# Early factors, one place for w2's sums, and loads in another order, in a decoder block's kernel

## The chip, the core and the metric

The kernel runs on one core of one Trainium2 chip. Its time is the device time of one execution in microseconds (us), given as the median of the runs; lower is better. The core's engines are TensorE (PE, matrix products; PEld is its loading of the stationary operand), VectorE (DVE), ScalarE (ACT) and GpSimd (POOL). SyncE (SP) issues most of the transfers; POOL issues others. An engine, and each DMA queue, takes its instructions in order.

## The reference

One layer over 2048 positions of width 1024: a mixer of dilated attention heads beside a gated recurrence, and a squared-ReLU MLP of width 4096, each between two norms.

```python
h = rms_norm(x, mix_norm_pre)
z = h @ w_in                                  # q, k, v, xr, gr
attn = dilated_attention(q, k, v)             # 8 heads of 64, three dilations, softmax-weighted
rec = rg_lru(causal_depthwise_conv(xr)) * gelu(gr)
x = x + rms_norm(concat([attn, rec]) @ w_out, mix_norm_post)
h = rms_norm(x, mlp_norm_pre)
a = relu(h @ w_ff_in)
x = x + rms_norm((a * a) @ w_ff_out, mlp_norm_post)
```

All is float32. `w_ff_in` is called w1 in the kernel, `w_ff_out` w2.

## The kernel before

**Precision.** A float32 operand is split into two parts, a high one (a cast to a shorter format on ACT, line 54) and a low one (the source minus the high part, mostly on DVE, line 55). A product takes three matmuls: high by high, high by low, low by high. The names end in H and L.

**Stages.** The 2048 positions are taken in two halves of 1024. TensorE does, in this order: the projections of half 0 with its attention and the recurrence; the last projections, the products q11, q12, q13 (LATER, line 1565), 24 matmuls per tile of q, k or v; the out-projection of half 0 (OutProj, tiles m, 634 to 728 us); the MLP's first product for half 0 (mlp_in, to 1056 us); its second (mlp_out) for half 0, mixed with the attention of half 1 (`interleave`, line 1304); the remaining sets of mlp_out while w_out is loaded again; then out-projection, mlp_in and mlp_out of half 1. From the out-projection of half 0 on PE's order is written by hand; in the attention of half 1 that of ACT, DVE and SP is too. Elsewhere a scheduler with a simulated time line orders the engines; `issue_after` gives it an instruction that must come first. On PE the change moves a few transposes in LATER and nothing else.

**mlp_in** computes `h @ w1` by Strassen's scheme, seven products (m = 1 to 7) for each of 16 column groups j. Each product's left factor f_m comes from the four quarters of w1's group: 1, 2, 3, 4 are made from single quarters (3 from a difference), 5, 6, 7 are sums (line 1009). The groups go in pairs of j (mlp_in_rest, line 1081), 14 products to a pair; a product here is 12 matmuls on 128x512. The right factors are the transposed activations: hHB and hLB (high and low), hHT and hLT (sums of them). Those of the last columns are made while the first products run, and the low parts hLT then take DVE.

After a group's products the output z is squared, and A = seven sums of z (tile as, lines 1061 to 1064) is stored in DRAM; beside it w2's own sums, tile w2s (function w2_sums, lines 1070 to 1075: a load of 1 MB, four sums, a store sb of 1 MB), are computed once, 16 times in half 0. The factors of j = 0, 1 and some of j = 2 are also stored in DRAM (scr["f"], sf) in half 0 and read back in half 1, instead of being made again (line 985 and below).

**Buffers.** Rings: sh.r, four buffers of 1 MB (z as sq, the sums as, w2s, and in half 1's attention k's two parts kh and kl); sh.w, five of 512 KB (w1's raw groups w1r, x, qs and qa); sh.pair and sh.s for split parts. A load for a ring waits on its queue until the buffer's last user is done.

**mlp_out** multiplies A's sums by w2's sums: seven factors m in the order 1, 6, 5, 3, 2, 7, 4 times 16 j, each a set of 12 matmuls. A set loads a (256 KB) and b (256 KB), casts on ACT (line 1227) and subtracts on DVE (line 1229). Four sets share the buffers, in turn, and the first four lie in another pool. In interleave `fill(n)` runs n quarters of sets between pieces of the attention of half 1. There each head has qs and kh, kl, vb loaded by SP (lines 429 to 445), qa copied from qs on DVE (line 433), va loaded by POOL (eight loads of 128 KB). The join of a head pair (lines 684 to 691: two products with the weights co and an addition, per half of the columns) is on DVE for the first three pairs, on POOL for the last; its result is stored to smix, which the out-projection loads as m_0, m_4 (mix_columns, line 787).

**load_w_out** (line 746) loads w_out row block by row block (512 KB each, woL), casts it and makes the low part; in half 1 each block comes between two calls of `between`, and each call runs one set.

## Time and profile before

| | us |
|---|---|
| median of 3 runs | 2286.15 (2276.22 to 2289.51) |
| the profiled execution, its span | 2279.51, 2277.7 |
| PE busy | 2180.9 (96%) |
| DVE, ACT, POOL busy | 1511.8 (66%), 1232.6 (54%), 461.2 (20%) |
| DMA | 466.15 MB, mean 205 GB/s |

In a timeline each line is one instruction: its start, its duration, engine, line of the kernel, operation, output <- inputs, and in brackets how long its engine had been idle before it and what ended the wait. SPq is SP's queue of transfers. A row of busy time by stretches gives, for a stretch from the span's start, each engine's busy time and its instructions, then the clock that TensorE was granted (1.00 is full), the mean busy share of the 16 DMA engines, and what they moved. A row of waits gives the total, the number and the longest. Tiles are named without their numbers.

### The profile page before, as it was taken

What the parts mean: (1) busy time and instruction counts of PE and PEld (TensorE: products, weight loads), DVE (VectorE), ACT (ScalarE), POOL (GpSimd) and SP (SyncE); (2) the same over time, 40 slices, a digit from 0 to 9 for tenths busy, and PEclk for the clock granted to TensorE, in tenths of its full rate; (3) what the DMA queues carried; (4) which work ended last, traced back from release to release, by engine and by line L of the source; (5) the groups of instructions that cost most, each with busy time, mean ns of one, the idle gap of its engine ahead of it and who ended that gap; (6) DMA issues with size and microseconds to landing.
All of it is one profiled execution on the core that took longest, in us unless ns stands there. A gap on an engine that the chain in (4) does not pass through costs nothing.

```text
span 2277.7 us, 30713 instructions
## 1 busy us (share of the span) xinstructions
PE 2180.9 (96%) x10264; PEld 1782.2 (78%) x10264; DVE 1511.8 (66%) x2900; ACT 1232.6 (54%) x2489; POOL 461.2 (20%) x549
## 2 busy tenths in 40 slices
PE   8999999989999899999899999898999999999998
PEld 6678878767788677787788887777878888888887
DVE  6757465877558777774667676777775656646556
ACT  7646464644334555454666666754454545654442
POOL 5543415454013201011001010122300000000003
PEclk9999999989999999999999999999999999999999
DMA  8365675635844577769777777868454444676665
GB/s 287 94 189 176 181 232 152 197 128 183 248 159 163 208 273 284 293 228 315 220 206 219 214 234 200 217 214 238 154 206 153 167 139 156 247 252 193 193 192 181
DMA packets 217550, 466.15 MB, mean 205 GB/s; under 512 B 22464, under 2 KB 77152, under 8 KB 211120
## 3 DMA queue, kind: packets, MB, share of 16 engines
q1 hardware_dynamic: 188624, 329.52, 46.6%
q0 software_dynamic: 28768, 134.66, 16.8%
q8 instruction: 81, 1.33, 0.2%
q14 instruction: 77, 0.63, 0.1%
HBM read 329.75 MB, written 151.13 MB: 211 GB/s over the span
## 4 chain that ended last, share of the span: by engine, by line
PE 64%; DMA 10%; DVE 9%; issue 6%; ACT 5%; POOL 1%; SPq 1%; DVEq 0%; POOLq 0%; ACTq 0%
PE o L1145 8%; PE o L1144 8%; PE o L1146 8%; PE z L198 3%; PE z L199 3%; PE z L200 3%; PE za L999 3%; PE za L998 3%; PE za L1000 3%; DMA w2s<-in_dram 3%; PE m L823 2%; PE m L821 2%; PE m L822 2%; PE zc L998 2%; PE zc L999 2%
## 5 line engine op out<-in xcount | busy, mean ns | idle before, releaser
L198 PE MATMUL z<-hH,wH 128*128 128x512 f32 x640 | 263.0, 411 | 18.6 <-ACT wH L54 8.2
L199 PE MATMUL z<-hL,wH 128*128 128x512 f32 x640 | 260.8, 408 | 0.3 <-DVE hL L173 0.3
L200 PE MATMUL z<-hH,wL 128*128 128x512 f32 x640 | 259.6, 407 | 0.0
L198 PEld LDWEIGHTS z<-hH,wH 128*128 128x128 f32 x640 | 122.5, 191 | 54.6 <-DVE xr L304 9.9
L199 PEld LDWEIGHTS z<-hL,wH 128*128 128x128 f32 x640 | 122.7, 192 | 30.7 <-issue 4.3
L200 PEld LDWEIGHTS z<-hH,wL 128*128 128x128 f32 x640 | 122.9, 192 | 30.3 <-issue 4.9
L409 ACT ACTIVATE smB<-smB,stB 128x128 f32<-128x128 f32 (+3 forms) x128 | 71.6, 561 | 80.4 <-DVE stB L403 80.2
L1003 ACT ACTIVATE sq<-sq 128x512 f32<-128x512 f32 x93 | 58.8, 632 | 88.4 <-DVE sq L1007 88.3
L55 POOL TENSOR_TENSOR wL<-wraw,wH 128x512 fp32r<-128x512 f32 x58 | 82.0, 1431 | 80.7 <-ACT wH L54 77.6
L1063 POOL DMA_DIRECT2D sa<-sq x31 | 16.5, 533 | 398.0 <-ACT sq L1004 397.8
L55 DVE TENSOR_TENSOR tlB<-pT_B,thB 128x384 fp32r<-128x384 f32 x96 | 57.1, 598 | 50.1 <-ACT thB L54 46.9
L54 ACT CAST wH<-wraw 128x512 fp32r<-128x512 f32 (+1 forms) x81 | 47.1, 612 | 66.6 <-DMA wraw<-in_dram 32.5
L409 ACT ACTIVATE sm<-sm,stA 128x256 f32<-128x256 f32 (+1 forms) x128 | 63.1, 495 | 30.7 <-DVE stA L403 30.4
L1004 ACT ACTIVATE sq<-sq 128x512 f32<-128x512 f32 x124 | 76.4, 629 | 2.2
L1074 DVE TENSOR_TENSOR w2s<-w2s 128x512 f32<-128x512 f32 x64 | 44.1, 689 | 33.0 <-DMA w2s<-in_dram 32.0
L1178 POOL TENSOR_TENSOR y<-y,g4b 128x512 f32<-128x512 f32 x8 | 12.4, 1578 | 259.5 <-ACT junk_y L84 259.5
L403 DVE CUSTOM_DVE_ANT_0 smB<-SB,mask_b 128x128 f32<-128x128 f32 (+3 forms) x128 | 59.4, 483 | 6.1 <-PE pT_B L377 5.4
L55 DVE TENSOR_TENSOR tlA<-pT,thA 128x512 fp32r<-128x512 f32 (+1 forms) x64 | 42.3, 669 | 26.6 <-ACT thA L54 26.2
L54 ACT CAST thB<-pT_B 128x384 fp32r<-128x384 f32 x96 | 48.5, 510 | 19.7 <-PE pT_B L377 10.6
L607 PE MATMUL oB<-thB,vb 128*128 128x256 f32 x192 | 49.1, 285 | 9.5 <-ACT thB L54 8.9
L821 PE MATMUL m<-woH,m_0H 128*128 128x512 f32 x128 | 51.7, 404 | 5.8 <-ACT m_0H L54 5.8
L998 PE MATMUL za<-hHT,f_6H 128*128 128x512 f32 x128 | 51.3, 401 | 5.5 <-ACT sq L1037 5.4
(577 smaller groups left out, 7083.5 us busy)
## 6 DMA issues: line engine op xcount, KB each, us to landing
sa<-as POOLq DMA_DIRECT2D x32, 1024.0 KB, 6.5
w1r<-in_dram SPq DMA_DIRECT2D x58, 512.0 KB, 4.2
sa<-sq POOLq DMA_DIRECT2D x31, 768.0 KB, 4.0
wraw<-in_dram SPq DMA_DIRECT2D x79, 256.0 KB, 3.6
w2s<-in_dram SPq DMA_DIRECT2D x16, 1024.0 KB, 7.7
sb<-w2s POOLq DMA_DIRECT2D x16, 1024.0 KB, 6.8
kh<-sk SPq DMA_DIRECT2D x24, 512.0 KB, 5.1
kl<-sk SPq DMA_DIRECT2D x24, 512.0 KB, 6.9
```

What stands on the lines that cost most here:

```text
L54: return (nc.scalar.copy(out=hi, in_=src), (lo_eng or nc.vector).tensor_tensor(out=lo, in0=src, in1=f32(hi), op=ALU.subtract))
L55: (lo_eng or nc.vector).tensor_tensor(out=lo, in0=src, in1=f32(hi), op=ALU.subtract))
L198: pe.matmul(z, hi[:, k, :], hh, start=(k == 0), stop=False)
L199: pe.matmul(z, hi[:, k, :], hl, start=False, stop=False)
L200: pe.matmul(z, lo[:, k, :], hh, start=False, stop=(k == KT - 1))
L409: s.activation(out=sm[:, c0:c0 + w], in_=sm[:, c0:c0 + w], func=AF.Exp, scale=-1.0, bias=st[:, 0, u, cols[j]:cols[j] + 1], accum_out=st[:, ...
L821: pe.matmul(o, mh, wh[:, ds], start=(k == order[0]), stop=False)
L998: pe.matmul(o, hi[:, k], bh[:, k], start=start and k == 0, stop=False, skip_group_check=True)
L999: pe.matmul(o, hi[:, k], bl[:, k], start=False, stop=False, skip_group_check=True)
L1144: pe.matmul(o, ah[:, ts], bh, start=fresh and j == 0, stop=False, skip_group_check=True)
L1145: pe.matmul(o, ah[:, ts], bl, start=False, stop=False, skip_group_check=True)
L1146: pe.matmul(o, al[:, ts], bh, start=False, stop=j == NJ - 1, skip_group_check=True)
```

## The change

Seven edits, in the order of the program.

1. Half 0's factors of j = 0, 1 are made during LATER, by a generator `early_factors` that is stepped five times after each product group, and stored. Half 0's mlp_in then reads them back, as half 1's does.
2. w2's sums for j = 2 to 15 use one buffer, place[0] (once for each group), and two further ones (w2x5, w2x9) the ring sh.r. They are placed behind the last made factor of the first pair (`sh.made`). The last A of half 0 uses that place too.
3. `first_loads`: q and the high part of k of half 1's first head are loaded before the last products of mlp_in; its low part follows the masks; qa is copied before the low part is loaded; va's loads come after the last store of A (`stored`).
4. The last four sets of mlp_out are loaded 16 to 20 sets early into buffers of sh.r, where k lay.
5. The last pair's join is on DVE, and its end runs after the fourth `between`.
6. load_w_out of half 1 loads all left column halves (256 KB each), then all right ones, two halves to a `between`.
7. For half 1 x, the gains and the norm's tiles are loaded after the first columns m, whose low parts are made on DVE for t = 0.

```diff
+def first_loads(nc, sh, scr):
+    qs = sh.px.tile([P, HT], F32R, tag="w", bufs=WB, name="qs1_0")
+    nc.sync.dma_start(out=f32(qs), in_=f32(scr["q"][1][0][0].rearrange("a c t -> c a t")))
+    kh = sh.px.tile([P, 2 * HT], F32R, tag="r", bufs=RB, name="kh1_0")
+    for x in range(2):
+        nc.sync.dma_start(out=f32(kh[:, x * HT:(x + 1) * HT]), in_=f32(twice(scr["k"][x][0][0, 0])))
+    return qs, kh
...
         for a, t in ((0, kh), (1, kl)):
+            if given and a == 0:
+                continue
+            if hf and a:
+                by_runs()
...
-        if hf:
-            by_runs()
...
+                with tc.issue_after(cst["stored"].ins) if hf else contextlib.nullcontext():
+                    (g if hf else nc.sync).dma_start(out=f32(va[cs, hf + 4 * i:hf + 4 * i + 4, :]),
...
-        e = v if amid else g
+        e = v if hf else g
...
-    for k in order:
+    parts = [slice(0, TB), slice(TB, D)]
+    for x, (ds, k) in enumerate([(ds, k) for ds in parts for k in order] if hf else [(slice(0, D), k) for k in order]):
         hi, lo = wo[k]
-        between()
+        if x % 2 == 0:
+            between()
...
-        split_there(nc, hi, lo, nc.gpsimd)
+        split_there(nc, hi, lo, nc.vector if hf and t == 0 else nc.gpsimd)
...
+def early_factors(nc, sh, scr, w1, j):
+    v, g = nc.vector, nc.gpsimd
+    raw = [sh.s(f"er{j}_{i}", (P, KH, P)) for i in range(4)]
+    a11, a12, a21, a22 = raw
+    for i, t in enumerate(raw):
+        nc.sync.dma_start(out=t, in_=w1[2 * j + i // 2][:, (i % 2) * KH:(i % 2 + 1) * KH])
+    yield
+    f = {}
+    def made(m, src=None):
+        if src is None:
+            split_there(nc, *f[m])
+        else:
+            f[m] = sh.pair(f"e{j}_{m}", (P, KH, P))
+            split(nc, *f[m], src)
+        for d, t in zip(scr["f"][j, m], f[m]):
+            g.dma_start(out=d, in_=f32(t).rearrange("p k t -> p (k t)"))
+    def sub(m, x, y, op=ALU.subtract):
+        f[m] = sh.pair(f"e{j}_{m}", (P, KH, P))
+        v.tensor_tensor(out=f32(f[m][1]), in0=x, in1=y, op=op)
+    sub(5, a21, a22, ALU.add)
+    sub(7, a11, a21)
+    sub(6, f32(f[5][1]), a11)
+    v.tensor_tensor(out=a21, in0=a12, in1=f32(f[6][1]), op=ALU.subtract)
+    made(7)
...
-            if hf and kept:
+            if kept and (hf or j < 2):
                 for d, t in kept:
                     nc.sync.dma_start(out=t, in_=d)
                 return
...
-            w2_sums(v)
+            w2_sums(v, place[0])
...
-        A = sh.r(f"as{n}")
+        A = place[0] if hf == 0 and j == NJ - 1 else sh.r(f"as{n}")
...
-    def w2_sums(e):
+    def w2_sums(e, W):
         j = todo.pop(0)
-        W = sh.r(f"w2s{j}")
         nc.sync.dma_start(out=W.rearrange("p (f a) d -> p f (a d)", f=2), in_=w2[2 * j:2 * j + 2].rearrange("f p d -> p f d"))
-        sums_right(lambda o, x, y, op: e.tensor_tensor(out=o, in0=x, in1=y, op=op), *[W[:, i] for i in range(4)])
+        with tc.issue_after(sh.made.ins):
+            sums_right(lambda o, x, y, op: e.tensor_tensor(out=o, in0=x, in1=y, op=op), *[W[:, i] for i in range(4)])
         g.dma_start(out=scr["b"][j], in_=W)
...
+            if not hf and i >= len(order) * NJ - 4:
+                if x == "a":
+                    t = sh.px.tile([P, 4, TB], F32R, tag="r", bufs=RB, name=f"r{n}")
+                hi, lo = [t[:, 2 * (x == "b") + k] for k in range(2)]
...
+            for k in {len(sets) - 20: (-2, -1), len(sets) - 14: (-4, -3)}.get(i, ()):
+                made[len(sets) + k] = load(*sets[k])
+            if 5 <= i < len(sets) - 7:
                 made[i + 3] = load(*sets[i + 3])
...
+            early = [early_factors(nc, sh, scr, w1, j) for j in range(2)]
+            for step in LATER.split():
+                run(step)
+                for _ in range(5):
+                    if early and next(early[0], True):
+                        early.pop(0)
...
+                first = first_loads(nc, sh, scr)
                 run_all(end)
+                cst["stored"] = sh.stored
...
-                wo = load_wo(1, lambda: [next(rest, None) for _ in range(4)])
+                calls = []
+                def between():
+                    for _ in range(4):
+                        next(rest, None)
+                    calls.append(0)
+                    if len(calls) == 4:
+                        run_all(last)
+                wo = load_wo(1, between)
```

How the order moves, at three places (L is the line in the file of its own kernel).

SP around the end of half 0's mlp_in, before (w2s and w1r are loads of w2 and w1, a0_1_0 the first set of mlp_out, sums of z; between the two pieces stand sets 1 to 7):

```order
L980 DMA w1r0_15_1_9320<-in_15_dram 128x1024
L1073 DMA w2s14_9345<-in_16_dram 128x2x1024
L1073 DMA w2s15_9397<-in_16_dram 128x2x1024
L1137 DMA a0_1_0_9546<-sa0_0_121 128x512
L1137 DMA b0_1_0_9548<-sw20_169 128x512
```

```order
L365 DMA mask_a1_9613<-in_19_dram 128x256
L367 DMA mask_b1_9615<-in_20_dram 128x512
L429 DMA qs1_0_9641<-sq1_0_75 128x1x1024
L440 DMA kh1_0_9642<-sk0_0_79 128x1x1024
L440 DMA kh1_0_9642<-sk1_0_83 128x1x1024
L440 DMA kl1_0_9643<-sk0_0_79 128x1x1024
L440 DMA kl1_0_9643<-sk1_0_83 128x1x1024
L1137 DMA a0_1_8L_9716<-sa0_8_129 128x512
L1137 DMA b0_1_8L_9719<-sw28_177 128x512
```

and after:

```order
L1042 DMA w1r0_15_1_9369<-in_15_dram 128x1024
L361 DMA qs1_0_9644<-sq1_0_75 128x1x1024
L1134 DMA place0_6282<-in_16_dram 128x2x1024
L364 DMA kh1_0_9646<-sk0_0_79 128x1x1024
L364 DMA kh1_0_9646<-sk1_0_83 128x1x1024
L1134 DMA place0_6282<-in_16_dram 128x2x1024
L1203 DMA a0_1_0_9596<-sa0_0_121 128x512
```

```order
L381 DMA mask_a1_9667<-in_19_dram 128x256
L383 DMA mask_b1_9669<-in_20_dram 128x512
L463 DMA kl1_0_9695<-sk0_0_79 128x1x1024
L463 DMA kl1_0_9695<-sk1_0_83 128x1x1024
L468 DMA vb1_0_9696<-sv0_0_87 128x8x128
L468 DMA vb1_0_9696<-sv1_0_91 128x8x128
L482 DMA va1_0_9752<-sv0_0_87 128x1x256
L1203 DMA a0_1_8L_9779<-sa0_8_129 128x512
```

q and kh have moved ahead of all of mlp_out's loads, between the last two loads into the single place; kl follows the masks, and the eighth set's loads now stand behind vb.

SP where mlp_out of half 0 ends (woL1 is w_out, m1_0_0L the out-projection's first columns), before:

```order
L756 DMA woL1_2_14233<-swo2_203 128x1024
L1137 DMA a0_4_14L_14444<-sa0_14_135 128x512
L1137 DMA b0_4_14L_14447<-sb14_167 128x512
L756 DMA woL1_3_14231<-swo3_204 128x1024
L1137 DMA a0_4_15L_14471<-sa0_15_136 128x512
L1137 DMA b0_4_15L_14474<-sb15_168 128x512
L830 DMA xt8_14630<-in_0_dram 128x1024
L830 DMA xt9_14692<-in_0_dram 128x1024
L812 DMA g2b1_0_14632<-in_3_dram 128x512
```

and after:

```order
L781 DMA woL1_7_14292<-swo7_208 128x512
L781 DMA woL1_0_14290<-swo0_201 128x512
L781 DMA woL1_1_14288<-swo1_202 128x512
L781 DMA woL1_2_14286<-swo2_203 128x512
L781 DMA woL1_3_14284<-swo3_204 128x512
L818 DMA m1_0_0L_14638<-smix1_104 128x4x128
L818 DMA m1_0_4L_14643<-smix1_104 128x4x128
L818 DMA m1_1_0L_14648<-smix1_104 128x4x128
L818 DMA m1_1_4L_14653<-smix1_104 128x4x128
L855 DMA xt8_14676<-in_0_dram 128x1024
```

The sets after j = 11 have gone from here; set 11 stands ahead of eight right halves of w_out, of which these are the last five, then come the columns m, and x and the gains behind them.

SP in the last projections (wraw is w_in's weights, er0 and er1 w1's quarters for the early factors, m0 the first columns of half 0's out-projection), before:

```order
L110 DMA wraw1_10_0_5809<-in_6_dram 128x512
L110 DMA wraw1_10_1_5813<-in_6_dram 128x512
L794 DMA m0_0_0L_6132<-smix0_103 128x4x128
L794 DMA m0_0_4L_6137<-smix0_103 128x4x128
L794 DMA m0_1_0L_6142<-smix0_103 128x4x128
L794 DMA m0_1_4L_6147<-smix0_103 128x4x128
L812 DMA g2b0_0_6178<-in_3_dram 128x512
```

and after:

```order
L993 DMA er0_0_5657<-in_15_dram 128x512
L993 DMA er0_1_5658<-in_15_dram 128x512
L993 DMA er0_2_5659<-in_15_dram 128x512
L993 DMA er0_3_5660<-in_15_dram 128x512
L110 DMA wraw1_10_0_5851<-in_6_dram 128x512
L110 DMA wraw1_10_1_5855<-in_6_dram 128x512
L235 DMA sq1_2_77<-zh1_2_0_5726 64x512 x2
```

The four quarters of j = 0 stand ahead of product 10's weights, and the columns m0 and the gains have moved behind all the remaining weights.

More of the change, by code (lines that the diff above doesn't have):

```diff
@@ L349, in scr_cols, with twice, attention @@
     return t[:, b * TB:(b + 1) * TB]
[L352 removed]
+def twice(t):
+    row, *rest = [list(x) for x in t.ap]
+    return bass.AP(t.tensor, t.offset, [row, [0, 2], *rest])
+def first_loads(nc, sh, scr):
[5 more added lines that the diff above has]
+    return qs, kh
+def attention(tc, p, bank, cst, scr, hf, mask_a_d, mask_b_d, pj, pw=None, px=None, first=None):
     nc = tc.nc
@@ L1348, in interleave @@
             ends.append(ending())
+            last = ends[-1]
     while ends:
         fill(1)
+    return last
 FIRSTFILL = 32
```

83 lines of the change are left out of this document (47 added, 36 removed).

## The prediction

> **What bounds the kernel now.** I read the page's engine totals first, then the busy time by stretches, then TensorE's own timeline where a stretch falls short.
>
> ```profile
> PE 2180.9 (96%) x10264; PEld 1782.2 (78%) x10264; DVE 1511.8 (66%) x2900; ACT 1232.6 (54%) x2489; POOL 461.2 (20%) x549
> ```
>
> The profiled execution took 2279.51 us, its span 2277.7. TensorE (PE) is idle for 2277.7 - 2180.9 = 97 us; that, and the matmuls that ran at half the clock, is all that an edit without fewer matmuls can win.
>
> ```profile
> core 0: us, PE busy (x) PEld busy (x) DVE busy (x) ACT busy (x) POOL busy (x), PEclk, DMA share, GB/s
> 585.00:634.00 49.00, 46.52 (x203) 36.84 (x201) 17.15 (x26) 11.78 (x20) 5.07 (x4) 1.00 0.68 193
> 634.00:728.00 94.00, 94.00 (x445) 78.42 (x444) 64.18 (x150) 40.98 (x108) 29.05 (x31) 1.00 0.48 163
> 750.00:800.00 50.00, 42.59 (x164) 32.41 (x162) 41.37 (x68) 31.66 (x59) 11.14 (x21) 0.93 0.59 214
> 800.00:1056.00 256.00, 251.56 (x1091) 204.17 (x1091) 186.39 (x297) 139.39 (x248) 20.85 (x40) 1.00 0.74 274
> 1056.00:1090.00 34.00, 26.32 (x112) 21.50 (x111) 10.65 (x21) 5.62 (x10) 6.58 (x12) 0.90 1.01 319
> 1510.00:1557.00 47.00, 36.96 (x150) 29.15 (x148) 37.52 (x58) 27.54 (x50) 16.14 (x19) 0.90 0.97 311
> 1650.00:1700.00 50.00, 48.14 (x214) 38.49 (x214) 37.20 (x67) 26.97 (x53) 2.97 (x4) 1.00 0.55 179
> ```
>
> Idle time: 2.5 us late in the projections, none in the out-projection, 7.4 at the start of half 0's mlp_in, 4.4 in the rest of it, 7.7 where attention of half 1 begins and 10.0 where mlp_out of half 0 ends. The last two have the DMA engines full (1.01 and 0.97). The last row is the start of mlp_in for half 1, where the factors of j = 0 and 1 are read back: 1.9 us idle. TensorE's waits in these stretches:
>
> ```profile
> 753.83 0.49 PE L999 MATMUL za<-hLT,f_6H 128*128 128x512 f32 x1 [1.46 <-DVE hLT L55]
> 765.26 0.50 PE L999 MATMUL za<-hLT,f_5H 128*128 128x512 f32 x1 [2.31 <-DVE hLT L55]
> 794.20 0.51 PE L998 MATMUL za<-hHT,f_6H 128*128 128x512 f32 x1 [2.28 <-ACT sq L1037]
> ...
> 1086.21 0.58 PE L524 MATMUL S<-kh,qa 128*128 128x256 f32 x1 [7.68 <-DVE qa L433]
> 1093.76 0.93 PE L377 MATMUL pT<-ident,sm 128*128 128x128 f32 x4 [1.89 <-ACT sm L409]
> ...
> 1531.18 0.79 PE L1144 MATMUL o<-b_10H,a_10H 128*128 128x512 f32 x1 [3.65 <-ACT b_10H L1227]
> 1557.38 0.80 PE L821 MATMUL m<-woH,m_0H 128*128 128x512 f32 x1 [5.81 <-ACT m_0H L54]
> ```
>
> Each number in brackets is idle time and what ended it. Only the time of these matmuls counts; the work elsewhere lies beside TensorE.
>
> **Early factors: the move to the projections.** The 14 factors of j = 0, 1 are computed amid the last three projection products. Their cost there, by the rows of these operations now:
>
> ```profile
> L54 ACT CAST f_6H<-ws x4: 604/614/622, 751.2 to 783.7; 128x512 fp32r<-128x512 f32 x4
> L55 DVE TENSOR_TENSOR f_6L<-ws,f_6H x4: 684/687/690, 754.3 to 786.3; 128x512 fp32r<-128x512 f32 x4
> ...
> PE z L198 <- ACT wH L54: 2.4, 1, 2.4
> ```
>
> 14 casts x 0.61 = 8.6 us of ACT, 22 subtractions and sums x 0.69 = 15.2 of DVE. In 585 to 634 these engines have 37 and 32 us free, so nothing of this reaches TensorE. DMA is dearer: 2 MB of loads and 7 MB of stores (28 x 256 KB from POOL). The 49 us moved 193 GB/s; at the 319 that the full stretch reached there is room for 126 x 49 = 6.2 MB, so some 3 MB spill into the out-projection, which runs at 163 GB/s and idles nowhere. Four of the loads (1 MB, 3.3 us at 319 GB/s) stand ahead of the weights of the product after next, which can move the one wait here (2.4 us, on such weights) or add one; but the columns of the out-projection and its gains no longer stand ahead of the last products' weights. I take 0, bounds -2.5 (that wait goes) to +6 (3.3 in each of two products).
>
> **Early factors: what mlp_in gains.** Ahead of the first wait DVE has no gap:
>
> ```profile
> 750.00:760.00 10.00, 7.78 (x25) 5.46 (x24) 10.00 (x18) 7.04 (x14) 2.17 (x4) 0.83 0.35 130
> 760.00:770.00 10.00, 7.09 (x23) 4.93 (x22) 10.00 (x18) 9.04 (x18) 4.26 (x8) 0.83 0.44 156
> ```
>
> hLT (the transposed activations' low part) is late because DVE also makes sums and low parts for 14 factors, 15.2 us within some 60. These go, and the start becomes half 1's, which already reads the factors. Two workings: idle plus clock is 7.4 + 0.07 x 50 = 10.9 now against 1.9, a gain of 9.0; and 164 matmuls where half 1 has 214 lack 50 x 50/214 = 11.7 us. I take -10; bounds -12 and -7, the latter if the 28 reads (7 MB in place of 2) come late, though DMA is at 0.59 here and half 1 lives with the same at 0.55.
>
> **w2's sums in one place.** The sums leave the ring of four buffers that z and the A sums use (the wait at 794.20 is for that ring), so the 4.4 us of idle in 800 to 1056 shrink. But 14 of 16 now share one buffer: each load waits on SP for the store before it, with loads of w1 and of set 1 queued behind, and DVE waits for the load.
>
> ```profile
> L1074 DVE TENSOR_TENSOR w2s<-w2s x64: 682/691/694, 795.2 to 1040.6; 128x512 f32<-128x512 f32 x64
> DMA to landing us min/median/max: 4.8/7.3/10.8
> ...
> sb<-w2s POOLq DMA_DIRECT2D x16, 1024.0 KB, 6.8
> ...
> DVE w2s L1074 <- DMA w2s<-in_dram: 32.0, 14, 5.8
> ...
> SPq L1073 <- DMA sa<-sq: 146.5, 11, 18.5
> ```
>
> One cycle is 7.3 (load) + 4 x 0.69 + 0.5 (issue) + 6.8 (store) = 17.4 us. TensorE spends 14 products of 12 matmuls on two j: (1056 - 800)/1091 x 168 = 39.4 us, 19.7 per j. So the chain fits by 2.3 us a cycle. SP stood up to 18.5 us before such a load already, and DVE up to 5.8, with no long wait of TensorE in this stretch. I take -2; bounds -5, and +10 if landings lengthen by a tenth in some cycles.
>
> **Head 0's q and k ahead.** TensorE waited 7.7 us for qa, a copy that DVE made after two low parts of set 8, whose loads SP issued late:
>
> ```profile
> 1061.33 1.42 SPq L440 DMA_DIRECT2D kh<-sk  x2
> 1075.09 1.17 SPq L440 DMA_DIRECT2D kl<-sk  x2
> 1076.36 0.54 SPq L1137 DMA_DIRECT2D a_8L<-sa  x1
> ...
> sa<-as POOLq DMA_DIRECT2D x2, 1024.0 KB, 13.8
> va<-sv POOLq DMA_DIRECT2D x8, 128.0 KB, 7.4
> kh<-sk SPq DMA_DIRECT2D x2, 512.0 KB, 16.0
> ```
>
> kl stood 13.8 us on SP, and kh took 16.0 to land in full DMA. Now q (0.5 MB) and kh (1 MB) are loaded before the stretch, qa no longer follows set 8, and va's eight loads come after the last store. 1.5 MB less at 319 GB/s is 4.7 us earlier. The wait for qa should go; but set 8's load still waits until TensorE leaves set 4 (four sets share the buffers), lands some 7 us later (as va's) and feeds a cast and a low part, so set 8 is late next: I leave 4 of 11.5 us (7.7 + 1.9 idle, and some 1.9 of half clock: 0.90 in 34 us is 6.8 us at half, about 3 of them inside the wait). So -7.5; bounds -11 (all but the exponent's wait), -3 (bytes alone decide and the clock still falls).
>
> **The end of mlp_out.** Two waits: set 10 (3.65, and 0.85 for its low part) and the first columns of the out-projection (5.81).
>
> ```profile
> 1525.90 2.96 POOL L684 TENSOR_TENSOR na<-na,co 128x512 f32<-128x512 f32 x2 [4.30 <-DMA co<-sco]
> ...
> 1526.19 3.23 DVE L55 TENSOR_TENSOR woL<-woL,woH 128x512 fp32r<-128x512 f32 x2 [2.07 <-ACT woH L54]
> 1531.15 1.61 DVE L1229 TENSOR_TENSOR b_10L<-b_10L,b_10H 128x512 fp32r<-128x512 f32 x1
> 1536.57 0.68 DVE L1229 TENSOR_TENSOR a_11L<-a_11L,a_11H 128x512 fp32r<-128x512 f32 x1
> ...
> 1530.50 0.62 ACT L1227 CAST b_10H<-b_10L 128x512 fp32r<-128x512 f32 x1 [1.90 <-DMA b_10L<-sb]
> 1540.49 0.32 SPq L1137 DMA_DIRECT2D a_15L<-sa  x1
> 1545.93 0.38 SPq L794 DMA_DIRECT2D m_0L<-smix  x1
> 1556.73 0.60 ACT L54 CAST m_0H<-m_0L 128x512 fp32r<-128x512 f32 x1
> ```
>
> Four sets (2 MB) are loaded some 15 sets earlier, and w_out's halves need fewer bytes before the first product. 2 MB at 311 GB/s is 6.4 us less in the full stretch. m_0 no longer stands behind x and the gains (1545.93 against 1540.49: 5.4 us), nor its cast behind four squares: it could be ready 6 to 8 us sooner, so the 5.81 goes; the three halves at set 10 load as many bytes per set as before, so half of its 4.5 may stay. Idle 10.0 and, at a clock of 0.90, some 4 for matmuls at half speed are 14; I take -8.5; bounds -13 and -2. The early sets have a price: their buffers are k's, and SP would stand before them if a head still read k; that is in the bound.
>
> The last join goes from POOL to DVE: six operations, 0.69 each on DVE, 4.1 us, where DVE has 9.5 free in 47. The DVE rows above are slow (1.61 each) while POOL adds, and 0.68 behind it: that saving is 2 x 0.9 on set 10. [...]
>
> **The sum:** 0 - 10 - 2 - 7.5 - 8.5 = -28, so 2279.5 - 28 = 2251.5 against the profiled execution. The median shown is 2286.15, 6.6 above it; half of that is added: 2255.
>
> **Rivals.** (1) The two full stretches are set by bytes in flight, and what is taken out of them is replaced by what was queued behind: their waits change place (set 8 and set 10 in turn for qa and m_0). For it: DMA shares of 1.01 and 0.97, and the 16.0 us of a 512 KB load. Against it: 3.5 MB do leave them. Then mlp_in's -10 and -2 stay and 2 us in each: -16, 2267. [...]
>
> (2) The single place sets the pace of half 0's mlp_in: slower. If landings lengthen, DVE stands at each load, and behind it stand the late factors that TensorE needs next. It decides from the point where 13 cycles eat the 28 us won: 19.7 + 28/13 = 21.9 us a cycle; at the longest load with a median store (20.9) the loss is 16, total 2271; with both near their longest, 23 us, it is 3.3 x 13 = 43 against 28: 15 slower, 2298. For it: DMA at 0.74 throughout and loads of 10.8. Against it: it takes the median cycle to rise by 4.5 us.
>
> (3) The moved work does nothing for mlp_in, since hLT waits for ACT and transposes as well: 0 - 2 - 7.5 - 8.5, 2265. Against it: half 1's start. That the change does not do what it says I leave aside; the order shows all the moves.
>
> **Chances:** forecast 0.58; (1) 0.20; (2) beyond its point 0.13; (3) 0.05; more than the forecast, towards 2236, 0.04. The likeliest case alone is 2246 to 2271: the terms' bounds, as independent, add to 7 below and 16 above (roots of the squares' sums: 2.5, 2, 3, 3.5, 4.5 and 6, 3, 12, 4.5, 6.5), and 2 more below for the choice of time. All cases: 2238 to 2284, which leaves out most of (2) and little below. 0.5% is about what runs of this kernel can tell from none: 11.4 us, 2274.7 to 2297.6. Faster holds the forecast, most of (1) and (3): 0.75; within: 0.15; slower: 0.10.
>
> **What would show it.** Right: DVE not full in 750 to 770 and no wait for hLT; no wait for qa near 1086, S starting when set 7 ends; m_0's cast ahead of the squares and TensorE idle for less than 2 us before the out-projection; DVE at 0.69 throughout the last join. Wrong: waits of DVE for the single place above 5 us with TensorE's waits for factors 3, 4 or 6 spread over 800 to 1056 (rival 2); waits of the same length for set 8 and set 10, with DMA still full (rival 1); a wait of more than 3 us for weights before 634 (early factors).

## The result and the profile after

| | before | after |
|---|---|---|
| median, us | 2285.54 (6 runs, 2276.22 to 2290.59) | 2258.48 (6 runs, 2255.71 to 2266.22) |
| ratio, 95% interval | | 0.9899 (0.9878 to 0.9921) |
| profiled execution, its span | 2279.51, 2277.7 | 2260.29, 2258.5 |

The change makes the kernel faster: by 1.0% as the ratio has it, 18 to 28 us by its interval; the medians lie 27.1 us apart, near the upper end. The two profiled executions differ by 19.2 us. The rest of the 27.1 is that the profiled execution of before lies 6.0 below its median and that of after 1.8 above. Only the 19.2 can be taken apart by stages.

From the page of the changed kernel, TensorE's totals (busy, share of the span, instructions):

```profile
PE 2173.0 (96%) x10264; PEld 1778.9 (79%) x10264; DVE 1508.6 (67%) x2908; ACT 1232.9 (55%) x2489; POOL 449.6 (20%) x541
```

Idle time fell from 97 to 2258.5 - 2173.0 = 85.5 us, and PE's busy time by 7.9. In both traces the granted clock is 1.00 or 0.50 (0.981 and 0.984 in the mean); it is 0.50 for 85.3 us before and 71.5 after, and PE is busy in 64.9 and 57.2 of these. A matmul on 128x512 starts every 0.43 us at 0.50 and every 0.23 at 1.00, so by estimate 3.6 of the 7.9 are matmuls that no longer run at half the clock. Where the time went, the busy time by stretches of the changed kernel shows (columns as before: busy time of PE, PEld, DVE, ACT and POOL, the clock, DMA share, GB/s):

```profile
585.00:634.00 49.00, 45.08 (x187) 36.27 (x186) 23.83 (x39) 14.63 (x26) 14.97 (x27) 0.93 0.95 310
634.00:728.00 94.00, 94.00 (x444) 78.26 (x443) 64.51 (x150) 40.79 (x108) 28.51 (x26) 1.00 0.56 187
750.00:760.00 10.00, 8.84 (x39) 6.85 (x38) 10.00 (x18) 7.20 (x14) 0.00 (x0) 1.00 0.57 177
760.00:770.00 10.00, 9.59 (x43) 7.61 (x42) 9.82 (x17) 7.79 (x16) 0.54 (x1) 1.00 0.24 80
750.00:800.00 50.00, 48.43 (x210) 38.98 (x209) 39.17 (x64) 31.46 (x57) 3.20 (x6) 1.00 0.63 228
800.00:1056.00 256.00, 256.00 (x1116) 208.82 (x1115) 184.09 (x298) 136.47 (x244) 26.19 (x49) 1.00 0.75 280
1056.00:1090.00 34.00, 27.44 (x128) 22.69 (x127) 13.30 (x34) 14.81 (x34) 0.55 (x1) 0.85 0.87 241
1475.00:1500.00 25.00, 22.41 (x125) 18.48 (x124) 19.06 (x40) 14.01 (x29) 0.00 (x0) 0.93 0.46 148
1510.00:1557.00 47.00, 42.55 (x178) 34.11 (x178) 30.59 (x65) 24.78 (x48) 8.39 (x10) 0.96 0.89 262
```

The start of half 0's mlp_in (750 to 800) now has 1.6 us of idle time where 7.4 were, and a full clock. From 800 to 1056 TensorE never stops (4.4 us before). Three stretches are short of that. The last projections (585 to 634) got worse: 3.9 us idle where 2.5 were, the clock at 0.93, with DMA at 310 GB/s in place of 193. The start of half 1's attention still has 6.6 us idle, in one piece. The end of mlp_out (1510 to 1557) has 4.4 where 10.0 were, but the stretch ahead of it has a new stop. TensorE's waits in the changed kernel (waiting line, what it waited for: us in total, times, longest):

```profile
PE z L198 <- DVE zn L228: 3.9, 1, 3.9
...
PE za L1060 <- ACT sq L1099: 1.2, 1, 1.2
...
PE o L1210 <- ACT b_8H L1293: 6.6, 1, 6.6
...
PE o L1210 <- ACT b_10H L1293: 3.4, 1, 3.4
PE pst L661 <- DVE sa L654: 2.6, 1, 2.6
```

The waits for hLT's first columns, qa and m_0 (2.31, 7.68 and 5.81 us in the profile of before) are gone or under half a microsecond. The wait for zn is new. The wait for set 8 stands where that for qa stood. Set 10 is as late as before (3.4 against 3.65). The wait of pst for sa was 1.0 and is 2.6.

To see gains and losses apart, the same matmul (by its count from the start, the order on PE being nearly the same) was looked up in both traces. The table gives how much sooner (negative) or later each stage gets through than in the trace of before; the bounds are times of before, and the sum is that of the last matmul. Every kernel run below is in it, with one trace each.

| kernel | 534-634 last projections | 634-728 out-projection | 728-810 mlp_in, start | 810-1056 mlp_in, rest | 1056-1107 attention, start | 1475-1652 end of mlp_out, out-projection | elsewhere | sum |
|---|---|---|---|---|---|---|---|---|
| the change | +6.0 | -0.1 | -10.4 | -4.6 | -2.4 | -4.4 | -3.1 | -19.0 |
| no_early | 0.0 | 0.0 | -3.7 | -4.1 | -4.5 | +0.9 | -1.8 | -13.2 |
| w2_ring | +2.2 | -0.1 | -8.3 | -0.5 | -2.8 | -1.9 | -2.1 | -13.5 |
| no_first | +5.2 | -0.1 | -10.2 | -4.8 | +1.8 | -1.7 | +3.2 | -6.6 |
| vb_behind | +2.2 | -0.1 | -10.6 | -4.8 | -0.5 | -5.5 | -1.8 | -21.1 |
| sets_first | +3.3 | -0.1 | -11.0 | -2.5 | -4.9 | -2.1 | -5.2 | -22.5 |
| er_late | +6.3 | +7.9 | -10.9 | -4.8 | -3.5 | -4.8 | -2.4 | -12.2 |
| r_hold | +3.0 | -0.1 | -10.2 | -4.8 | -2.1 | -7.7 | -1.8 | -23.7 |
| wo_later | +4.6 | -0.1 | -10.9 | -4.8 | -2.1 | -6.4 | -2.2 | -21.9 |
| best1 | +2.2 | +1.0 | -10.7 | -3.4 | -5.4 | -9.2 | +2.5 | -23.0 |
| best2 | +13.4 | -0.1 | -10.5 | -4.8 | -4.7 | -10.0 | -2.1 | -18.8 |
| join_pool | +3.4 | +0.9 | -10.2 | -4.8 | -2.8 | -1.7 | -0.9 | -16.1 |
| no_last4 | +4.4 | -0.1 | -10.0 | -4.8 | -2.5 | -8.4 | +0.9 | -20.5 |

Kernels that share a stage's code show its scatter: +2.2 to +6.0 (mean 3.7) in the last projections, -2.1 to -4.5 at the start of attention, +0.9 to -5.5 (mean -2.8) at the end of mlp_out, -5.2 to +3.2 elsewhere, under 1 in the others but for single traces. A difference inside these bounds is read from the waits, if at all. Single runs of before lay between 2270.74 and 2290.59, so a single time tells no difference of a few us; it is given with each experiment all the same.

Two places need a closer view. At the start of attention, in the changed kernel's timeline:

```profile
1048.64 2.49 SPq L468 DMA_DIRECT2D vb<-sv  x2
1051.18 9.64 SPq L482 DMA_DIRECT2D va<-sv  x1
1060.92 2.85 SPq L1203 DMA_DIRECT2D a_8L<-sa  x1
...
1064.77 0.28 PE L546 MATMUL S<-kh,qa 128*128 128x256 f32 x1
...
1070.68 0.62 ACT L1293 CAST a_8H<-a_8L 128x512 fp32r<-128x512 f32 x1 [22.95 <-DMA a_8L<-sa]
...
1071.97 0.80 PE L1210 MATMUL o<-b_8H,a_8H 128*128 128x512 f32 x1 [6.56 <-ACT b_8H L1293]
```

S begins as soon as set 7 ends (1064.55), with no wait. But SP issues vb and the one load of va that is its own (the other eight are POOL's), which are needed later, ahead of set 8, and that load of va holds SP for 9.64 us. Set 8's load goes out at 1060.92 and arrives at 1070.68. In the last projections:

```profile
588.52 3.10 SPq L993 DMA_DIRECT2D er<-in_dram  x2
591.71 3.62 SPq L236 DMA_DIRECT2D sq<-zl  x2
...
602.68 0.69 DVE L55 TENSOR_TENSOR zl<-zn,zh 128x512 fp32r<-128x512 f32 x1 [10.62 <-DMA sq<-zl]
603.48 0.69 DVE L228 TENSOR_TENSOR zn<-z,bc 128x512 f32<-128x512 f32 x1
604.22 0.79 PE L198 MATMUL z<-hH,wH 128*128 128x512 f32 x1 [3.92 <-DVE zn L228]
```

DVE stands for 10.62 us: its next zl overwrites one whose store sq went out behind two loads of the early factors, in DMA that is now 0.95 full. The copy zn, which frees TensorE's accumulator, stands behind it on DVE.

### The profile page after: what moved, and what is told of

The parts are those of the page before. It is cut to its first block, busy times and chain, and to the rows that moved or that the text cites. A ratio compares the mean times of both kernels' runs of the same rounds, so it can differ in the third digit from the quotient of the medians.

```text
span 2258.5 us, 30786 instructions
## 1 busy us (share of the span) xinstructions
PE 2173.0 (96%) x10264; PEld 1778.9 (79%) x10264; DVE 1508.6 (67%) x2908; ACT 1232.9 (55%) x2489; POOL 449.6 (20%) x541
## 4 chain that ended last, share of the span: by engine, by line
PE 72%; DVE 8%; DMA 7%; issue 4%; ACT 4%; SPq 1%; POOL 0%; DVEq 0%; ACTq 0%; POOLq 0%
PE o L1210 8%; PE o L1211 8%; PE o L1212 7%; PE za L1061 5%; PE za L1062 5%; PE za L1060 5%; PE z L198 3%; PE z L199 3%; PE z L200 3%; PE m L846 3%; PE m L848 3%; PE m L847 3%; PE zc L1061 2%; PE zc L1062 2%; PE zc L1060 2%
## 5 line engine op out<-in xcount | busy, mean ns | idle before, releaser
L1244 POOL TENSOR_TENSOR y<-y,g4b 128x512 f32<-128x512 f32 x8 | 12.4, 1579 | 259.4 <-ACT junk_y L84 259.4
L629 PE MATMUL oB<-thB,vb 128*128 128x256 f32 x192 | 48.6, 282 | 11.3 <-ACT thB L54 10.4
L393 PE MATMUL pT_B<-ident,smB 128*128 128x128 f32 x320 | 52.2, 279 | 2.6 <-DVE tlB L55 1.8
L414 DVE CUSTOM_DVE_ANT_0 sm<-S,mask_a 128x256 f32<-128x256 f32 (+1 forms) x128 | 47.4, 409 | 9.1 <-PE pT L393 4.0
L1061 PE MATMUL za<-hLT,f_5H 128*128 128x512 f32 x128 | 50.1, 391 | 2.0 <-DVE hLT L55 2.0
```

What stands on the lines that cost most here:

```text
L414: v.tensor_tensor_reduce(out=sm[:, c0:c0 + w], in0=sp[:, c0:c0 + w], in1=mask[:, mask.shape[-1] - w:], scale=1.0, scalar=3.0e38, op0=ALU.a ...
L1061: pe.matmul(o, hi[:, k], bl[:, k], start=False, stop=False, skip_group_check=True)
```

## The experiments

Each edit is made to the changed kernel; none leaves out any of the computation. "Before" is a run of the kernel before on the same chip.

### Without the early factors

```diff
...
-            if kept and (hf or j < 2):
+            if hf and kept:
...
-            early = [early_factors(nc, sh, scr, w1, j) for j in range(2)]
...
```

Half 0 makes the factors of j = 0 and 1 from w1 again, in mlp_in (the first quarters are loaded into the single place); w2's sums stay in that place.

> The changed kernel without the early factors: half 0 makes the 14 factors of j = 0, 1 in mlp_in again, from w1 (the first quarters lie in the single place). Theory 1 (making them amid mlp_in's start was what kept DVE full): TensorE's idle time in the first 50 us of mlp_in comes back from 1.6 us to 6 or more, with waits for hLT; the waits in the last projections (3.9 for zn, 1.7 for wH) shrink to about the 2.4 of before; in total some 4 us slower than the changed kernel, about 2264. Rival (the start was relieved by w2's sums standing later on DVE): the start stays below 3 us of idle, and the total falls to about 2253 because the projections lose their waits.

2267.17 us, before 2290.17. The busy time by stretches and, of the waits, those at the start of mlp_in:

```profile
750.00:760.00 10.00, 7.78 (x25) 5.45 (x24) 10.00 (x18) 7.51 (x15) 2.16 (x4) 0.83 0.28 105
760.00:770.00 10.00, 7.04 (x22) 4.88 (x21) 10.00 (x18) 8.08 (x16) 5.17 (x10) 0.83 0.58 211
750.00:800.00 50.00, 44.83 (x177) 34.85 (x176) 41.56 (x69) 33.36 (x62) 11.25 (x21) 0.93 0.60 224
```

```profile
PE za L1062 <- DVE hLT L55: 4.2, 2, 2.8
```

The wait for hLT and the clock of 0.83 are back, nearly to the row (before: 7.78 and 7.09 us busy). So the factors did make hLT late: they are worth 10.4 - 3.7 = 6.7 us of the start's gain, and the remaining 3.7 come without them. The loss in the last projections is gone with them, 0.0. Their net gain by stages is about 6.7 - 3.7 (the mean cost) = 3 us. That nothing would come of it (rival 3) is refuted, and so is the cost of nothing in the projections.

### w2's sums back in the ring

```diff
-            w2_sums(v, place[0])
+            w2_sums(v, sh.r(f"w2s{j}"))
...
-        A = place[0] if hf == 0 and j == NJ - 1 else sh.r(f"as{n}")
+        A = sh.r(f"as{n}")
```

> The changed kernel with w2's sums, and the last A, back in the ring of four buffers. Theory 1 (the ring's places are what z waited for): waits of PE's first f_6 product for the copy of z come back, about 4 to 7 us between 790 and 1056, total 2263 to 2265. Rival (they went because the early factors relieved ACT and DVE): still no wait of TensorE in 800 to 1056, total within 3 us of the changed kernel.

2265.71 us, before 2290.17. The waits of TensorE in mlp_in, up to 805 us and behind it:

```profile
PE za L1060 <- ACT sq L1099: 2.8, 3, 1.2
...
PE za L1060 <- ACT sq L1099: 2.0, 2, 1.0
PE zc L1060 <- DVE sq L1069: 1.1, 2, 0.6
```

The waits for z's copies, which need a buffer of the ring, are back: 5.9 us against 1.2. The two mlp_in stages lose 10.4 + 4.6 - 8.3 - 0.5 = 6.2. So the ring was short of a buffer, as the prediction had it, and the place is worth some 6 us, spread over both stages.

The chain in the place never set the pace. The changed kernel's page (KB each, us from issue to landing) and DVE's waits for the place:

```profile
place<-in_dram SPq DMA_DIRECT2D x14, 1024.0 KB, 7.2
sb<-place POOLq DMA_DIRECT2D x14, 1024.0 KB, 5.3
```

```profile
DVE place L1136 <- DMA place<-in_dram: 12.5, 10, 3.1
```

The loads and stores grew shorter, not longer (7.7 and 6.8 on the page of before). A cycle is 7.2 + 2.8 + 0.5 + 5.3 = 15.8 us, and DVE's wait is 3.1 at most, where it was 5.8. Rival 2 is refuted, by 6 us a cycle against its point of 21.9.

### Without the loads ahead

```diff
-                first = first_loads(nc, sh, scr)
+                first = None
```

Head 0's q and k are loaded in turn; va still waits for the last store.

> The changed kernel with q and kh of the first head loaded where they were; va still after the last store. Theory 1 (the loads ahead only moved the wait from qa to set 8): the wait for qa comes back with 5 to 8 us, that for b_8H falls below 2, and the stretch from 1050 to 1100 loses as much as with the change, within 3 us; total within 4 us of 2258. Rival (the move is worth something by itself): the stretch loses 5 us or more beyond the changed kernel's 9.8, total about 2264.

2272.61 us, before 2290.17. In the timeline, the two longest waits of TensorE:

```profile
1071.14 0.55 PE L546 MATMUL S<-kl,qa 128*128 128x256 f32 x1 [3.91 <-DMA kl<-sk]
...
1082.66 1.18 PE L393 MATMUL pT<-ident,sm 128*128 128x128 f32 x4 [2.52 <-ACT sm L420]
```

The wait for qa, which was expected back, does not return. S waits 3.9 us for k's low part instead, set 8's first product 1.8 for its cast, and the transposes 2.5 for the exponents. The stage is 1.8 us slower than before, 4.2 behind the change: that is what the loads ahead are worth, and not the 7.5 of the prediction, since set 8 took 6.6 of it back. The trace is 12.4 us behind the change's; 6.3 of that lie in the column "elsewhere", and the runs do not show why. The next two experiments ask why set 8 is late.

### vb behind sets 8 and 9; all values behind sets 8 to 11

The first lets vb's two loads go out behind sets 8 and 9 and SP's load of va behind set 9, the second puts all loads of va and vb on SP behind set 11.

```diff
+        for _ in range(3 if given else 0):
+            yield
         for x in range(hf + 1):
```

```diff
...
+                hold = first is not None and pr == u == 0 and not env.get("go")
+                if hold:
+                    env["n"] = env.get("n", 0) + 1
+                    if env["n"] > 2:
+                        return env[u]
...
+                env["va"] = values_a(pr, nc.sync)
+                head(0)()
...
```

> The changed kernel, with the first head's vb and the first piece of va issued on SP behind the loads of sets 8 and 9, as they were before, q and kh still ahead. Theory 1 (set 8 is late because SP stood 9.6 us in the issue of va's piece behind 1 MB of vb): a_8L is issued when TensorE leaves set 4, near 1057, lands by 1064; the wait for b_8H falls from 6.6 to below 2 us, little half clock, total about 2251. Rival (bytes in flight, not the order on SP): a_8L is issued sooner but takes over 12 us to land, the wait stays above 4, total above 2256.

> The changed kernel with all of the first head's vb and its pair's va (the eight pieces too, on SP instead of POOL) issued behind the loads of sets 8 to 11. Theory 1 (set 8, and in the run before this one set 10 ahead of the exponents, wait for what stands before them on SP): no wait over 2 us from 1050 to 1085, the loss of that stretch falls from 9.8 to about 3, total about 2251; the first product with va, near 1086, does not wait more than 2. Rival (the transfers of that stretch are one sum that has to be paid at some wait): the wait comes back at the first product with va or at set 11 or 12, 4 us or more, total above 2255.

The first: 2258.13 us, before 2290.17. Its timeline:

```profile
1061.12 4.96 SPq L484 DMA_DIRECT2D va<-sv  x1
1066.18 0.71 SPq L1205 DMA_DIRECT2D a_10L<-sa  x1
...
1073.73 0.62 ACT L1295 CAST a_10H<-a_10L 128x512 fp32r<-128x512 f32 x1 [4.17 <-DMA a_10L<-sa]
...
1076.31 1.18 PE L393 MATMUL pT<-ident,sm 128*128 128x128 f32 x4 [4.07 <-ACT sm L420]
```

Set 8's wait fell from 6.6 to 2.3 us, so its place behind the values was the cause. But va now holds SP ahead of set 10; ACT, in order, waits for that set's cast with the softmax's exponents behind it, and TensorE for these, 4.07 us. The stage is 1.9 worse than in the change's trace.

The second: 2256.76 us, before 2281.11. Its waits:

```profile
PE oA L582 <- DMA vb<-sv: 2.8, 1, 2.8
PE pT L393 <- DVE na L409: 2.2, 1, 2.2
```

No set is late. Now the values are, by 2.8 us. The stage gains 4.9, more than in any trace with the change's order (2.1 to 4.5), 2.5 more than in its own; best1 and best2 below, which have the same order, gain 5.4 and 4.7. The three traces with this order are 2.2 us better in the mean than the eight with the change's (5.0 against 2.8). So 2 to 2.5 of the 6.6 us could be had by order alone, and the rest changed place twice, as rival 1 has it.

### Early factors of j = 1 behind the last weights

```diff
...
-            early = [early_factors(nc, sh, scr, w1, j) for j in range(2)]
+            early = [early_factors(nc, sh, scr, w1, j, (lambda: tc.issue_after(pj.last_w.ins)) if j else None) for j in range(2)]
...
```

> The changed kernel with the early factors of j = 1 loaded only behind the last weights of the projections; j = 0 as in the change. Theory 1 (DVE stood 10.6 us for the store of z's low part, which was queued on SP behind the quarters of j = 1 in full DMA, and the next product's copy of z stood behind that): the wait for zn (3.9) near 604 goes, the loss from 560 to 634 falls from 10.3 to below 5; the columns m of the out-projection may come late by up to 4 us at 634. Rival (POOL's stores of the factors of j = 0 fill the DMA engines): the wait near 604 stays above 2.5.

2267.0 us, before 2281.11. The waits in the last projections and at the start of the out-projection:

```profile
PE z L198 <- DVE e_7L L1009: 2.2, 1, 2.2
PE z L198 <- DVE zn L228: 2.0, 1, 2.0
...
PE m L846 <- ACT m_0H L54: 3.2, 1, 3.2
```

The stop at 604 us is gone. A wait of 2.0 for zn ends at 630.6 instead, and behind 638 TensorE waits 2.3 us for DVE's vs ahead of a transpose and 3.2 for the out-projection's first columns. The 2.2 us for e_7L, one of DVE's early sums, is not this edit's: three traces of the change's own code in this stage (sets_first, r_hold, join_pool) have 2.0 to 2.8 us of it, beside 1.7 to 2.6 for zn. The two stages lose 6.3 and 7.9, against 6.0 and -0.1; the first is about the most that other traces of the changed code lose there, the second stands in no other trace. Late bytes were no cheaper here than early ones: they met the loads of the stage behind.

### The last four sets: held, or loaded in turn

In the changed kernel, the early sets' splits and the stop of pst:

```profile
1490.28 1.24 ACT L1293 CAST r<-r 128x512 fp32r<-128x512 f32 x2 [1.66 <-DMA r<-sa]
1491.54 0.58 ACT L408 COPY fold<-oB 64x512 f32<-64x512 f32 x1
...
1490.93 1.31 DVE L1295 TENSOR_TENSOR r<-r 128x512 fp32r<-128x512 f32 x2 [2.03 <-ACT r L1293]
1493.96 0.47 PE L661 MATMUL pst<-sel,sa 128*16 128x32 f32 x8 [2.59 <-DVE sa L654]
```

ACT waits for a set that TensorE takes 38 us later (its first matmul starts at 1528.49), and the copy fold of the last head and, behind it, sa and pst stand there too. The first experiment holds the splits of the four sets behind those of set 8 of m = 4; the second loads these sets in turn, into the buffers that the others use.

```diff
...
+            with tc.issue_after(held[k].ins) if late else contextlib.nullcontext():
...
```

```diff
-            if not hf and i >= len(order) * NJ - 4:
+            if False:
...
-            if 5 <= i < len(sets) - 7:
+            if 5 <= i < len(sets) - 3:
```

> The changed kernel with the casts and low parts of the last four sets held behind those of the set 8 before the last on their engines. Theory 1 (the wait for pst near 1494, 2.6 us against 1.0 before, comes from ACT waiting for the early sets' load ahead of the fold of the last head): that wait falls to about 1.0 and the half clock after it goes, 2 to 4 us less, total about 2255. Rival (it comes from the fuller DMA or DVE as such): the wait stays above 2.

> The changed kernel with the last four sets loaded in their turn, not early; w_out's halves, the order of the columns m and the join as in the change. Theory 1 (the early sets bring the end forward because 2 MB leave the full stretch, and cost the wait at pst): the wait for pst falls from 2.6 to 1.0, set 10 waits as before, and between set 12 and the out-projection waits of 3 us or more come back; from 1475 to 1600 within 3 us of the change. Rival (the order of the columns ahead of x, the gains and the squares alone took the 5.8 us away): no wait after set 11, pst at 1.0, the total 3 to 5 us below the changed kernel.

Held: 2255.86 us, before 2281.11. Pst waits 1.0 us again, as before the change, and the stage gains 7.7; set 9's low part is late in its place (4.1 us). In turn: 2258.76 us, before 2280.93. Its waits from 1480 to 1560:

```profile
PE o L1211 <- DVE b_9L L1295: 1.8, 1, 1.8
PE o L1210 <- ACT b_10H L1293: 1.7, 1, 1.7
PE pst L661 <- DVE sa L654: 1.0, 1, 1.0
```

Without the early sets the stage gains 8.4, beyond every trace that has them as the change does (+0.9 to -5.5), and about as much as with their splits held (7.7 here, 9.2 and 10.0 in best1 and best2). Sets 9 and 10 together wait about as long as set 10 did with them, and nothing waits behind set 11. So the early sets bring nothing in this stage, and their splits, where the change has them, cost some 4 us of it; the single time, 2258.76, is no lower than the change's median. What took m_0's 5.81 away the traces show, ACT's first square (before) and m_0's cast (after):

```profile
1550.29 1.06 ACT L84 ACTIVATE junk_y<-y 128x1024 bf16<-128x1024 f32 x1 [4.75 <-DVE y L1154]
...
1528.57 0.62 ACT L54 CAST m_0H<-m_0L 128x512 fp32r<-128x512 f32 x1 [0.26 <-DMA m_0L<-smix]
```

Before, m_0's load went out at 1545.93 and took 4.5 us to land, but its cast stood on ACT behind four squares, the first of which waited for the last set's result, and ran at 1556.73. Now it runs ahead of them (the first square is at 1538.27) and TensorE starts at 1539.38 without a wait. That is edit 7. What w_out's halves (edit 6) are worth was not run by itself.

### w_out one step later

```diff
+                between()
                 wo = load_wo(1, between)
```

> The changed kernel with w_out's first halves loaded one set later. Theory 1 (set 10 is late because its loads share the DMA engines and ACT's order with w_out's halves): the wait at set 10 (3.4 us for b_10H, 0.9 for its low part) falls by 1 to 3 us; the first product of the out-projection does not wait, since m_0 had 5 us. Rival (set 10 waits for the turn of its buffers): unchanged, within 0.5 us.

2257.31 us, before 2281.11. TensorE's waits for sets 9 to 11 add to 1.9 + 0.2 + 0.8 + 0.6 = 3.5 us in place of 3.4 + 0.9, and the clock stays at 1.00 from 1500 to 1550 (the changed kernel: 0.97). The stage gains 6.4, a little beyond the scatter: sets wait less when w_out's halves start later, but only a little.

### The last join on POOL

```diff
-        e = v if hf else g
+        e = v if amid else g
```

> The changed kernel with the last pair's join on POOL again, at its new place in the program. Theory 1 (POOL's additions slow DVE's operations of two inputs from 0.69 to about 1.6 us, and the casts' low parts of sets 9 to 11 stand there): some six operations of DVE beside POOL's take 1.2 to 2 us each, the wait at set 10 grows by 1 to 2 us, the sum of smix comes later and m_0 with it; 2 to 4 us slower than the changed kernel. Rival (DVE has the room, nothing waits for it): DVE's operations slow down, yet the total stays within 1.5 us.

2263.15 us, before 2276.74 (median of 11). In the timeline:

```profile
1520.43 3.57 DVE L55 TENSOR_TENSOR woL<-woL,woH 128x512 fp32r<-128x512 f32 x2 [1.67 <-ACT woH L54]
1523.52 1.61 POOL L713 TENSOR_TENSOR na<-na,nb 128x512 f32<-128x512 f32 x1
1523.92 1.75 DVE L1295 TENSOR_TENSOR a_10L<-a_10L,a_10H 128x512 fp32r<-128x512 f32 x1
1525.60 0.68 DVE L1295 TENSOR_TENSOR b_10L<-b_10L,b_10H 128x512 fp32r<-128x512 f32 x1
```

Beside POOL's additions DVE takes 1.75 us and 3.57 for two, and 0.68 as soon as POOL is done; with the join on DVE every such operation in this stretch took 0.62 to 0.69. Set 10's low part is late by 3.2 us (0.9 in the changed kernel). The stage gains 1.7, which is inside the scatter, so the 2.7 us that lie between this gain and the change's 4.4 are not shown to be the join's; the durations and the wait are.

### Two versions put together

best1 has the values behind sets 8 to 11, the held splits and w_out one step later. best2 adds that the early factors of j = 0 are made during the recurrence, ahead of the last projections.

```diff
...
+            for step in BETWEEN.split():
+                run(step)
+                for _ in range(2):
+                    next(early[0], None)
...
```

> The changed kernel with three edits at once: the first head's va and vb behind sets 8 to 11 on SP, the splits of the last four sets held in the order of the sets, w_out's first halves one set later. Theory 1 (the three act at different places, so their gains add: about 5 at 1065 to 1090, 3 at 1494, 2 at sets 9 and 10): 8 to 12 us below the changed kernel, 2247 to 2251, ratio to the kernel before about 0.985. Rival (each gain is given back at the next wait): within 4 us of 2257.

> The run before, and the early factors of j = 0 made amid the recurrence's last four products, ahead of w_out's load, those of j = 1 over the three products after. Theory 1 (what the early factors cost in the projections is the crowd of loads and stores on SP and in the DMA engines from 560 to 605, which begins with w_out's 4 MB): the loss from 560 to 634, 10.3 us, falls to 4 to 6, total another 4 us lower, ratio about 0.983. Rival (the crowd only moves into the recurrence, whose products wait there): the same total as the run before, within 3 us.

With the kernel before at 2276.74 us on the same chip, best1 took 2254.47 (6 runs), a ratio of 0.9891 (0.9867 to 0.9914), and best2 2260.56 (6 runs), 0.9930 (0.9912 to 0.9948). best1 gains 5.4 and 9.2 us in the two stages that it mends, but its ratio isn't told apart from the change's 0.9899 (0.9878 to 0.9921), as its rival expected. best2, expected 4 us below best1, is 6 above it: it loses 13.4 in 534 to 634: TensorE waits 11.7 us there for weights, whose loads stand behind those of the early factors (three of these hold SP for 8.24 us, from 583.80). To make them sooner did not hide their bytes: this is what its rival expected, and more. best1's order without the early sets was not run.

## Why the prediction was right, and where not

The forecast case holds: faster by 27 us in the medians, 2258.48 against 2255. For the profiled execution the sum was too hopeful by 9 us: -19 where -28 was worked out, and 3.1 of the -19 lie in stages that no edit touches, so the five terms gave some -16. The median came nearer than that because that of before, over six runs, lay 6 us above its profiled run (3.3 were added) and that of after 1.8 below. That nearness is luck; the direction is not.

- **Early factors in the projections: 0 was taken, with +6 as a bound; measured +2.2 to +6.0, mean 3.7.** The step that failed is "some 3 MB spill into the out-projection, which runs at 163 GB/s and idles nowhere", with the loads ahead of weights as its only price. The out-projection did take bytes without loss (187 GB/s, -0.1). But with DMA at 0.95 DVE had to wait for a store, and a copy behind it on DVE held TensorE (in four other traces in part an early sum on DVE). In the change's own trace the clock then was 0.93 over 49 us: 0.50 for 6.8 us from 603.3, with PE busy in 5.9 of them, which at 0.43 us a matmul for 0.23 is by estimate 2.7 of the 6.0. The text concluded from the room on ACT and DVE that "nothing of this reaches TensorE". They had the room; what was not counted is that DVE's own order ties it to loads and stores on SP's queue.
- **The start of mlp_in: -10 taken, -10.4 measured.** Both workings held: half 1's start was the right likeness. The factors are 6.7 of it; the other 3.7 come without them, 2.1 by w2_ring through the sums of w2, which the prediction had booked in the next term. One of its signs did not come: DVE was to be no longer full in 750 to 770, and is busy for 10.00 and 9.82 us of the two tens. What changed is the order of its work. Before, five operations for factors stood between 750 and 764.5, ahead of hLT's last part; now none does before 765.48, and hLT is done by 761.8 (765.2 before).
- **w2's sums: -2 taken, -4.6 measured in 810 to 1056, some 6 by undoing it alone.** The mechanism was right (z's copies waited for the ring), the size taken too small: all 4.4 us of idle time went, not half. The fear beside it, a chain of 17.4 us in 19.7, never came near: 15.8.
- **Head 0's q and k: -7.5 taken, -3 as the bound of "bytes alone decide"; measured -2.4 (-2.1 to -4.5).** The wait for qa went, and the text named set 8 as what is late next, but it priced that, together with the rest that stays, at "4 of 11.5 us". It was 6.6, and the clock fell with it (0.85 in 1056 to 1090). The failed step is the reason given for the lateness: not the buffer of set 4, but vb and va on SP ahead of set 8, one issue of 9.64 us. Before, set 8 went out ahead of them (1076.36 against 1077.42 for vb and 1082.19 for SP's load of va); with q and k gone from that place, the values moved up into it. The text followed the loads that move, and not those that follow them on SP. A reading beside it was off too: kl stood 12.2 us on SP, for the store of a sum A in the buffer that it takes; the 13.8 count from kh's issue. In its outcome rival 1 was right here.
- **The end of mlp_out: -8.5 taken, bounds -13 and -2; measured -4.4, and -2.8 as the mean of seven traces.** m_0's 5.81 went, as worked out. "2 MB less in the full stretch" did not help set 10 (3.4 against 3.65), and the price of the early sets was looked for on SP, where k's buffers are freed; it lay on ACT and DVE, which stand for them in order ahead of the last head's copies. The join on DVE did what its rows said (0.68 us an operation); what that saves in time is inside the scatter.
- **Rivals.** 2 and 3 fell. 1 was right in its outcome where attention starts and, for set 10, at the end: in vb_behind, sets_first, r_hold and er_late a wait that was removed came back elsewhere, in part. It was wrong for m_0 and hLT, whose causes were the order on ACT and on DVE and not bytes.

Not settled: why the last projections lose 2.2 in one trace and 6.0 in another of the same code, what edit 6 is worth, and the 3 us that the change's trace gains in stages that no edit touches.

## What to carry to other kernels

A load that is moved early is paid for by whatever stands behind it in order: behind its issue on the queue (set 8, behind 9.64 us of va), and behind its first user on an engine (the copy fold, behind a cast that waited 1.66 us); write down both before counting its bytes. In a stretch where DMA is full, mend the order of what is needed first, and expect the wait to come back in part at the next consumer (here 6.6 us at set 8, then 4.1 at the exponents or 2.8 at the values). Work that left a full engine (DVE at the start of mlp_in, 10.4 us for the 10 taken) or a short ring (w2's sums, 4.6 where 4.4 were idle) gave what its idle rows said, and more reliably than bytes moved between stretches (2.4 for 7.5).

## What the runs showed of the hardware

- Issuing itself took long in four traces. SP spent 9.64 us on one load of va in the changed kernel and 4.96 in vb_behind, 6.53 on a set's load in no_first and 8.24 on three loads of the early factors in best2, where most loads of a set took 0.32 to 0.43. Around these issues the DMA share was 1.04 in the changed kernel and 0.9 or more in vb_behind, and what stood behind on SP went out after them: a_8L at 1060.92 in the changed kernel, a_10L at 1066.18 in vb_behind. All but best2's stand right behind a load of vb; whether vb's loads have a part in it beside the full DMA the runs do not tell.
- Half the clock came in pieces of few lengths. In the traces of before and after it lasts 3.41 us (12 times), 6.83 (13) or 10.24 (2), apart from the last piece of each. In the changed kernel it begins at 1067.5, 2.0 us into the wait of 6.56, and lasts 10.24 us, 5.7 of them behind the wait; after pst's 2.59 it lasts 3.41. Before, it lasts 3.41 from 755.4, where TensorE had waited 1.46 us and, 0.5 us later, 0.70. The length of a wait does not decide alone: before, waits of 2.28 us (ending at 794.20) and 2.45 (on weights, ending at 599.73) were followed by a clock of 1.00 (794 to 800, and 599.73 to 634).
